# Filter products in high and low halves, vector work moved from GpSimd to VectorE, in a two-layer hybrid backbone

## The chip, the cores and the metric

One core of a Trainium2 chip runs the kernel. The metric is device time in microseconds (us) for one execution, the median of several. The core has TensorE (PE, matmuls; PEld its weight loads), VectorE (DVE), ScalarE (ACT), GpSimd (POOL), and SyncE (SP), which here only issues transfers (DMA). Every engine works off its own instructions in their order and waits for the others on semaphores.

## What is computed

Two layers act on 512 latent and 256 context tokens of 1024 channels. Each layer modulates a norm with vectors computed from a conditioning vector, projects, runs three mixers side by side (a long convolution called Hyena, neighbourhood attention, latent attention "MLA"), projects back, and runs an MLP with squared ReLU. The parts that the change touches:

```python
def _modulation(cond, w_mod, b_mod):
    m = jax.nn.silu(cond) @ w_mod + b_mod
    return jnp.split(m[:, None, :], 6, axis=-1)

def _adaln(h, g, shift, scale):
    return _rms(h, g) * (1.0 + scale) + shift

def _hyena_filters(L, w1, b1, w2, b2, w3, b3, freq):
    ...
    hdn = jnp.sin(freq[0] * (z @ w1.astype(F32) + b1.astype(F32)))
    hdn = jnp.sin(freq[1] * (hdn @ w2.astype(F32) + b2.astype(F32)))
    h = (hdn @ w3.astype(F32) + b3.astype(F32)).reshape(L, HY_ORDER, 2, HY_DIM)
    ...
    h = h * decay[:, None, None, :]
    return h / (jnp.sum(jnp.abs(h), axis=(0, 2), keepdims=True) + EPS)
...
        mx = _modulation(c, w_mod[i], b_mod[i])
        mc = _modulation(c_ctx[None], w_mod[i], b_mod[i])
        px = _adaln(x, g_norm1[i], mx[0], mx[1]) @ w_in[i]
        pc = _adaln(cx, g_norm1[i], mc[0], mc[1]) @ w_in[i]
```

## The kernel before

**Layout and precision.** Activations lie with channels on partitions: `xT` is 8 tiles of 128 channels by 768 tokens (512 latent, then 256 context). Large products are made from high and low halves: `split` (L135) copies a tile to fp32r on ScalarE (L136) and subtracts that from the source on VectorE (L137); `gemm` (L295) and `mm3` (L131 to L133) then run three matmuls, high-high, high-low and low-high. Matmuls on plain f32 tiles run as two recorded passes.

**Order.** A planner orders each engine's instructions by their place in the program and by when it expects them to be ready; generators woven together (`weave`, `fill`) set that place. Pools reserve memory; a tile with `bufs=n` turns over n buffers.

**Start** (from L1164). `filter_hidden` loads its small tables and computes two sine layers for both layers' filters at once, each as one piece of 768 columns (`sin_layer`): ScalarE scales, five VectorE operations reduce the argument, ScalarE takes the sine. SP then issues x (8 transfers), the last filter weight `w3`, the decay and Fourier tables, and 16 blocks of 512 KB of modulation weights (13 buffers). The squares of x are summed between the two sine layers (`sumsq`). Then three things are woven: the rstd and the multiplication of x by it (`norm_x`), `modulation(0, 1)` and `(0, 0)` (scale and shift of the first norm, matmuls L150), and `spectra`, the filters' generator: per 128 tokens a product with `w3` (L372, plain f32, 65 rows), the decay and norm sums on VectorE, ScalarE and GpSimd (L375 to L385), and per filter a Fourier product (L409). After that `norm_h` makes `hh` (ScalarE, L252) and `hl` (VectorE L253, then GpSimd subtracts, L254). The first large product (`mla_in`, L295) and the value projection (`na_v`, L131 to L133) take the rest of `spectra` as filling.

**Attention and the rest of the modulation.** `mla_attend` of layer 0 is woven with `modulation(0, 2)` and `(0, 4)`. The other modulation vectors come from `modulation_rows` (L174): per block of 128x1024 weights, two streams (latent, context). GpSimd multiplies the block by the context row (L189); one step later VectorE multiplies the block by the latent row and sums (L193) and ScalarE sums GpSimd's product (L194). (0,3), the shift of the second norm, (0,5) and all six vectors of layer 1 run in this way, 64 blocks, one per step of the fill: one per output tile m in the output projection (L1355 on), then `MD + 2` = 3 more (L1379), because L1382 needs (0,3) for the first MLP product, and the others inside `mlp`, `FR` of them per ff1 tile of the first chunks and one per pair of ff2 tiles. In the output projection VectorE also adds the gated tile to x (`add_gated`, L1059), which frees TensorE's tile, makes the low half (L1376) and sums squares (L217).

**Layer 1's norm** (`norm_stream`, L257): per tile of one stream VectorE multiplies (L263), ScalarE makes the high half (L264), VectorE the full value (L265), GpSimd the low half (L266). `na_v` of layer 1 waits for it.

## Time and profile before

| | us |
|---|---|
| median of 3 runs | 1859.73 |
| lowest, highest | 1854.02, 1862.49 |
| the profiled execution, whole time | 1861.99 |
| its span in the profile | 1860.1 |
| TensorE busy (share of the span) | 1770.8 (95%) |
| VectorE busy | 1227.3 (66%) |
| ScalarE busy | 807.1 (43%) |
| GpSimd busy | 339.4 (18%) |

The profile is of one execution. Its views used here: busy time by stretch, the instructions of an engine in order of time (equal ones merged), groups of instructions by line, and the list of waits. `out<-in` are the program's names, `xN` a count, and a bracket gives the idle time of the engine before an instruction and what ended it. A busy TensorE is not TensorE at its peak.

### The profile page before, as it was taken

The page shows a single profiled execution, that of the slowest core. Times are in us where ns is not written, and L with a number is a line of the kernel's source. Part 1 is how long each engine was busy: PE and PEld are TensorE (multiplying, and loading weights), DVE is VectorE, ACT ScalarE, POOL GpSimd, SP SyncE. Part 2 cuts the span into 40 slices and gives each one's busy share as a digit, 9 for nine tenths or more (in the row PEclk, how much of TensorE's full clock was granted, in tenths as well). Part 3 has the DMA queues.
Part 4 walks back from the last instruction along what each step waited for, and adds up shares of the span by engine and source line. Part 5 has one row for each costly group of instructions (what it writes and reads, how often), then busy time and mean ns, then how long its engine had stood idle before and what let it go on. Part 6 is the DMA issues. An engine that isn't in the chain of part 4 may idle for free. (4 is left out here: it accounts for less than half of the span.)

```text
span 1860.1 us, 27267 instructions
## 1 busy us (share of the span) xinstructions
PE 1770.8 (95%) x10794; PEld 1504.4 (81%) x10794; DVE 1227.3 (66%) x2111; ACT 807.1 (43%) x1355; POOL 339.4 (18%) x265
## 2 busy tenths in 40 slices
PE   6899988899998999999999999899899999999999
PEld 2688877666686878888888888789677799999997
DVE  5866876766668876665666447887876665555554
ACT  3433425566644643334333224554566652333231
POOL 1523321200043433233322000530300000000000
PEclk9999998999998999999999999899999999999999
DMA  9123423151243333333332222363040023223332
GB/s 339 60 85 134 161 95 101 42 207 56 100 160 126 114 136 130 120 114 136 113 136 102 69 68 88 96 202 132 24 177 24 24 93 100 91 91 95 98 91 79
DMA packets 73246, 205.07 MB, mean 110 GB/s; under 512 B 12540, under 2 KB 24589, under 8 KB 71840
## 3 DMA queue, kind: packets, MB, share of 16 engines
q1 hardware_dynamic: 71520, 198.10, 31.0%
q0 software_dynamic: 1600, 5.24, 0.8%
q8 instruction: 85, 1.39, 0.3%
q14 instruction: 41, 0.34, 0.1%
HBM read 181.30 MB, written 21.23 MB: 109 GB/s over the span
## 5 line engine op out<-in xcount | busy, mean ns | idle before, releaser
L295 PE MATMUL mm<-t,wh 128*128 128x512 f32 (+1 forms) x2496 | 495.2, 319 | 1.9 <-DVE t L1059 1.3
L295 PEld LDWEIGHTS mm<-t,wh 128*128 128x128 f32 x2496 | 373.2, 190 | 38.0 <-issue 2.4
L136 ACT ACTIVATE wh<-wr 128x1024 fp32r<-128x1024 f32 (+2 forms) x176 | 184.6, 1050 | 415.8 <-PE mm L295 394.4
L295 PE MATMUL mm<-t,wl 128*128 128x512 f32 (+1 forms) x1248 | 298.1, 317 | 0.0
L189 POOL TENSOR_TENSOR wmp<-wm,t 128x1024 f32<-128x1024 f32 x64 | 169.5, 2655 | 485.8 <-DMA wm<-in_w_modr_dram 308.8
L137 DVE TENSOR_TENSOR wl<-wr,wh 128x1024 fp32r<-128x1024 f32 (+2 forms) x176 | 228.0, 1296 | 37.3 <-ACT wh L136 33.8
L295 PE MATMUL mm<-ah,wh 128*128 128x512 f32 (+1 forms) x768 | 231.4, 355 | 4.1 <-DVE t L1059 3.5
L295 PE MATMUL mm<-al,wh 128*128 128x512 f32 (+1 forms) x768 | 233.5, 359 | 0.0
L295 PE MATMUL mm<-ah,wl 128*128 128x512 f32 (+1 forms) x768 | 232.0, 356 | 0.0
L1059 DVE SCALAR_TENSOR_TENSOR t<-mm,mods,t 128x512 f32<-128x512 f32 x216 | 135.9, 657 | 134.3 <-PE mm L295 127.5
L295 PEld LDWEIGHTS mm<-t,wl 128*128 128x128 f32 x1248 | 194.7, 189 | 16.5
L193 DVE SCALAR_TENSOR_TENSOR wm<-wm,t 128x1024 f32<-128x1024 f32 x64 | 91.0, 1426 | 102.7 <-POOL wmp L189 102.7
L295 PEld LDWEIGHTS mm<-ah,wh 128*128 128x128 f32 x768 | 126.7, 188 | 28.5 <-DVE t L1059 3.4
L295 PEld LDWEIGHTS mm<-ah,wl 128*128 128x128 f32 x768 | 127.6, 188 | 22.4
L295 PEld LDWEIGHTS mm<-al,wh 128*128 128x128 f32 x768 | 126.4, 188 | 20.2
L194 ACT ACTIVATE wmp<-wmp 128x1024 f32<-128x1024 f32 x64 | 67.9, 1060 | 149.8 <-POOL wmp L189 149.8
L137 DVE TENSOR_TENSOR al<-relu,ah 128x768 fp32r<-128x768 f32 (+1 forms) x64 | 68.2, 1066 | 37.1 <-ACT ah L136 37.1
L447 DVE TENSOR_REDUCE mmx<-mm 128x1 f32<-128x768 f32 (+1 forms) x80 | 67.7, 847 | 32.1 <-PE mm L133 31.5
L452 ACT ACTIVATE msb<-mm,mmx,qrs 128x768 f32<-128x768 f32 (+1 forms) x80 | 72.2, 903 | 25.3 <-DVE mmx L449 21.3
L1370 PE MATMUL mm<-t,wh 128*128 128x512 f32 x320 | 78.1, 358 | 1.6 <-DVE t L1059 1.6
L1023 ACT ACTIVATE mpt<-mm 128x768 f32<-128x768 f32 (+1 forms) x80 | 57.5, 725 | 49.7 <-PE mm L1022 49.6
L136 ACT ACTIVATE ah<-relu 128x768 fp32r<-128x768 f32 (+1 forms) x64 | 47.3, 739 | 63.4 <-DVE relu L1122 63.3
(311 smaller groups left out, 2990.1 us busy)
## 6 DMA issues: line engine op xcount, KB each, us to landing
wr<-in_w_ff_dram SPq DMA_DIRECT2D x128, 512.0 KB, 3.5
wm<-in_w_modr_dram SPq DMA_DIRECT2D x64, 512.0 KB, 4.4
wm<-in_w_mod_dram SPq DMA_DIRECT2D x32, 512.0 KB, 8.0
wr<-in_w_in_t_dram SPq DMA_DIRECT2D x18, 512.0 KB, 3.8
qk<-qk_spill SPq DMA_DIRECT2D x9, 576.0 KB, 6.2
qk_spill<-upk SPq DMA_DIRECT2D x12, 384.0 KB, 3.0
kx<-kk POOLq DMA_DIRECT2D x16, 256.0 KB, 2.5
wr<-in_w_in_qk_dram SPq DMA_DIRECT2D x8, 512.0 KB, 4.0
```

The costliest lines, as they stand in the source:

```text
L136: act.activation(hi, src, AF.Copy)
L137: dve.tensor_sub(lo, src, r32(hi))
L189: pool.tensor_tensor(P[i - MD], W[i - MD], cr[:, 1], ALU.mult)
L193: dve.scalar_tensor_tensor(w, w, 1.0, cr[:, 0], ALU.mult, ALU.mult, accum_out=mods[:, l, v, k, 0:1])
L194: act.activation(pr, pr, AF.Copy, accum_out=mods[:, l, v, k, 1:2])
L295: pe.matmul(out_[:, po:po + b - a], wk[wx], mk[mx][:, a:b], start=(k == 0 and i == 0), stop=(k == nk - 1 and i == 2))
L447: dve.tensor_reduce(mx, src, AX.X, ALU.max, negate=True)
L452: act.activation(sb[:, h, :n], src[:, h, :n], AF.Exp, bias=mx[:, h:h + 1], scale=1.0 if scale is None else scale[:, h:h + 1], accum_out=sm ...
L1023: act.activation(pt[:, 0:nkt, qt * 128:(qt + 1) * 128], tt[:, :nkt * 128].rearrange("p (c q) -> p c q", q=128), AF.Copy)
L1059: dve.scalar_tensor_tensor(xT[:, m, a:b], t[:, a:b], mods[:, l, v, m, s:s + 1], xT[:, m, a:b], ALU.mult, ALU.add)
L1370: pe.matmul(t[:, a:b], ws[wx], half[mx][:, k % 4, a:b], start=(k == ks[0] and i == 0), stop=(k == 7 and i == 2))
```

## The change

- `modulation_rows`: VectorE makes both streams' sums, in two passes over a block; GpSimd and ScalarE have no part. Weights are loaded two blocks ahead (`MD = 2`).
- The shift (0,3) is made during layer 0's `mla_attend`, with a `cond_rows` of its own; the forced steps at L1379 go. `FR` becomes one step per ff1 tile from the second chunk on. The `qk` tile of `mla_attend` has one buffer instead of two.
- Norms: `norm_x` and `norm_h` go; `norm_stream` serves both layers. VectorE multiplies, ScalarE scales in place, and `split` makes both halves.
- Filters: the sine layers run in three pieces of 256 columns. The hidden values of a layer fill one half of 128 rows with their high part and the other with their low part, and `w3` is stacked to match, so a filter product is two fp32r matmuls of 128 rows.
- Start: `w3`, decay and the first Fourier table are loaded ahead of x; the modulation's blocks have 10 buffers; the squares come after the sine layers, woven with `spectra` at 0.5, and the modulation after the rstd, woven at 1.0.

```diff
@@ modulation_rows
-            if item(i - MD):
-                ...
-                pool.tensor_tensor(P[i - MD], W[i - MD], cr[:, 1], ALU.mult)
-            if item(i - MD - 1):
-                ...
-                dve.scalar_tensor_tensor(w, w, 1.0, cr[:, 0], ALU.mult, ALU.mult, accum_out=mods[:, l, v, k, 0:1])
-                act.activation(pr, pr, AF.Copy, accum_out=mods[:, l, v, k, 1:2])
+        for i in range(MD):
+            weights(i)
+        for i, (l, v, k) in enumerate(items):
+            weights(i + MD)
+            w, junk = W.pop(i), p([128, 1024], tag="wmp")
+            for s in range(2):
+                dve.scalar_tensor_tensor(w if s else junk, w, 1.0, cr[:, s], ALU.mult, ALU.mult,
+                                         accum_out=mods[:, l, v, k, s:s + 1])
@@ norm_stream
         for k in range(KD):
-            t = p([128, NT], tag="sq", bufs=2)[:, a:b]
-            g, m = gains[:, l, 0, k, s:s + 1], mods[:, l, 0, k, s:s + 1]
-            dve.tensor_mul(xT[:, k, a:b], xT[:, k, a:b], rb[:, a:b])
-            act.activation(hh[:, k, a:b], xT[:, k, a:b], AF.Identity, bias=m, scale=g)
-            dve.tensor_scalar(t, xT[:, k, a:b], g, m, ALU.mult, ALU.add)
-            pool.tensor_sub(hl[:, k, a:b], t, r32(hh[:, k, a:b]))
+            t, g, m = xT[:, k, a:b], gains[:, l, 0, k, s:s + 1], mods[:, l, 0, k, s:s + 1]
+            dve.tensor_mul(t, t, rb[:, a:b])
+            act.activation(t, t, AF.Identity, bias=m, scale=g)
+            split(hh[:, k, a:b], hl[:, k, a:b], t)
+            yield
-    MD = 1
+    MD = 2
-    FR = (0, 2)
+    FR = 1
@@ filter_hidden
+        n = 256
+        s1 = {}
+        for c in range(4):
+            if c < 3:
+                t = b_tile()[:, 0:n]
+                pe.matmul(t, w1, z[:, c * n:(c + 1) * n], start=True, stop=True)
+                s1[c] = sin_layer(p, t, fb[:, 0:1], hyc, 0, n)
+            if c:
+                cs = slice((c - 1) * n, c * n)
+                t = b_tile()[:, 0:n]
+                pe.matmul(t, w2, s1.pop(c - 1), start=True, stop=True)
+                s2 = sin_layer(p, t, fb[:, 1:2], hyc, 1, n)
+                for l, (a, b) in enumerate(h2):
+                    mine, other, _ = filter_halves(l)
+                    act.activation(a[mine, cs], s2[mine], AF.Copy)
+                    dve.tensor_sub(a[other, cs], s2[mine], r32(a[mine, cs]))
+                    act.activation(b[mine, cs], s2[mine], AF.Copy)
             yield
+    def filter_weights(l, p):
+        ...
+        for x in (mine, other):
+            act.activation(hi[x], raw[mine], AF.Copy)
+        dve.tensor_sub(lo[mine], raw[mine], r32(hi[mine]))
+        act.activation(lo[r:r + 1], raw[r:r + 1], AF.Copy)
+        dve.tensor_sub(lo[r + 32:r + 33], raw[r:r + 1], r32(lo[r:r + 1]))
+        return hi, lo
@@ filter_unit
-                pe.matmul(ph, h2[:, (t0 + tt) * 128:(t0 + tt + 1) * 128], w3[:, o * 512:(o + 1) * 512],
-                          start=True, stop=True)
+                for i in range(2):
+                    pe.matmul(ph, h2[i][:, (t0 + tt) * 128:(t0 + tt + 1) * 128], w3[i][:, o * 512:(o + 1) * 512],
+                              start=(i == 0), stop=(i == 1))
@@ mla_attend
-                QK[hp] = p([128, 2, 6, 192], tag="qk", bufs=2)
+                QK[hp] = p([128, 2, 6, 192], tag="qk")
@@ mlp, ff1
-                for _ in range(FR[c] if c < 2 else 1):
+                for _ in range(FR if c else 0):
@@ start
-    weave((x_in(), 1.0), (chain(modulation(0, 1, wmp, ws=wm1), modulation(0, 0, wmp, ws=wm0)), 1.0), fill=(fill, 1.4))
+    weave((squares_in(), 1.0), fill=(fill, 0.5))
+    next(rstd)
+    weave((chain(modulation(0, 1, wmp, ws=wm1), modulation(0, 0, wmp, ws=wm0)), 1.0), fill=(fill, 1.0))
+    rb = next(rstd)
     wmp.close()
     ...
+    for _ in zip(norm_stream(0, 0, rb, xT, hh, hl, xp), norm_stream(0, 1, rb, xT, hh, hl, xp)):
+        pass
@@ layer 0, attention and output projection
-                  (chain(*[modulation(0, v, wmp) for v in (2, 4)]), 0.2))
+                  (chain(*[modulation(0, v, wmp) for v in (2, 4)]), 0.2),
+                  (modulation_rows([(0, 3)], cond_rows(wmp), wmp), 0.2))
...
-            fill = modulation_rows([(0, 3), (0, 5)] + [(1, v) for v in range(6)], cond_rows(wmp), wmp)
+            fill = modulation_rows([(0, 5)] + [(1, v) for v in range(6)], cond_rows(wmp), wmp)
...
-        if not last:
-            for _ in range(MD + 2):
-                next(fill)
```

## Rows read from the trace of the kernel before

**Rows 1.** Busy time by stretch: us; PE, PEld, DVE, ACT, POOL; PEclk, DMA share, GB/s.
```profile
50.00:55.00 5.00, 5.00 (x34) 2.35 (x33) 3.40 (x11) 1.01 (x2) 2.44 (x2) 1.00 0.00 0
...
75.00:80.00 5.00, 4.67 (x24) 3.75 (x23) 5.00 (x6) 5.00 (x10) 4.41 (x3) 1.00 0.00 0
...
490.00:500.00 10.00, 10.00 (x69) 7.58 (x68) 7.75 (x19) 7.70 (x13) 0.00 (x0) 1.00 0.00 2
...
700.00:750.00 50.00, 50.00 (x286) 43.70 (x285) 32.28 (x45) 21.00 (x32) 16.12 (x6) 1.00 0.35 127
```

**Rows 2.** TensorE in order of time, the start: start us, us, instruction, count.
```profile
34.60 2.08 PE L372 MATMUL b<-w,t 65*128 65x512 f32 x2
...
48.18 1.08 PE L150 MATMUL b<-wm,cst 128*32 128x256 f32 x8
...
58.19 1.07 PE L150 MATMUL b<-wm,cst 128*32 128x256 f32 x16
...
75.51 1.05 PE L295 MATMUL mm<-t,wh 128*128 128x512 f32 x4
...
139.74 1.02 PE L372 MATMUL b<-w,t 65*128 65x512 f32 x2
...
162.91 0.98 PE L295 MATMUL mm<-t,wh 128*128 128x512 f32 x4 [0.54 <-ACT t L489]
```

**Rows 3.** Groups by shape, 0 to 130 us: busy us, mean ns, idle before.
```profile
L254 POOL TENSOR_TENSOR t<-sq,t 128x768 fp32r<-128x768 f32 x8 | 16.3, 2032 | 3.3 <-DVE sq L253 1.8 <-PE b L409 1.6
...
L375 DVE TENSOR_TENSOR h<-b,t 128x512 f32<-128x512 f32 x18 | 12.3, 686 | 7.5 <-PE b L372 5.9 <-POOL sd L385 1.6
L253 DVE TENSOR_SCALAR sq<-t,gains,mods 128x256 f32<-128x256 f32 x8 | 12.0, 1501 | 0.0
...
L339 DVE SCALAR_TENSOR_TENSOR arg<-argk,arg 128x768 f32<-128x768 f32 x4 | 3.8, 954 | 0.1
```

**Rows 4.** TensorE in order of time, end of the output projection.
```profile
573.20 0.93 PE L1370 MATMUL mm<-t,wh 128*128 128x512 f32 x4 [1.62 <-DVE t L1059]
576.07 1.01 PE L1370 MATMUL mm<-t,wl 128*128 128x512 f32 x2 [1.95 <-DVE wl L137]
...
601.50 2.72 PE L224 MATMUL b<-ones,t 128*128 128x1 f32 x12 [5.22 <-DVE t L217]
604.08 1.63 PE L295 MATMUL mm<-t,wh 128*128 128x512 f32 x4
```

**Rows 5.** VectorE, GpSimd and SP in order of time, same stretch.
```profile
558.32 3.42 DVE L193 SCALAR_TENSOR_TENSOR wm<-wm,t 128x1024 f32<-128x1024 f32 x1
...
570.77 1.22 DVE L193 SCALAR_TENSOR_TENSOR wm<-wm,t 128x1024 f32<-128x1024 f32 x1
...
592.77 3.41 DVE L193 SCALAR_TENSOR_TENSOR wm<-wm,t 128x1024 f32<-128x1024 f32 x1 [5.45 <-POOL wmp L189]
...
590.34 4.75 POOL L189 TENSOR_TENSOR wmp<-wm,t 128x1024 f32<-128x1024 f32 x2 [15.41 <-DMA wm<-in_w_modr_dram]
...
576.04 9.70 SPq L280 DMA_DIRECT2D wr<-in_w_ff_dram  x3
```

**Rows 6.** Waits, 540 to 700 us: us in total, times, longest us.
```profile
PE mm L295 <- DVE t L1059: 3.5, 2, 3.1
```

**Rows 7.** Layer 1's norm: TensorE and ScalarE in order of time; L266's durations.
```profile
1168.57 0.29 PE L131 MATMUL mm<-wh,t 128*128 128x288 f32 x1
...
1198.84 3.18 PE L673 MATMUL b<-ones,csq 128*128 128x1 f32 x28
...
1165.88 2.92 ACT L264 ACTIVATE t<-t,mods,gains 128x512 fp32r<-128x512 f32 x4
...
L266 POOL TENSOR_TENSOR t<-sq,t x16: 762/1261/2641, 1166.8 to 1191.1; 128x512 fp32r<-128x512 f32 x8, 128x256 fp32r<-128x256 f32 x8
```

**Rows 8.** The costliest groups (part 5 of the page): one row of VectorE.
```profile
L193 DVE SCALAR_TENSOR_TENSOR wm<-wm,t 128x1024 f32<-128x1024 f32 x64 | 91.0, 1426 | 102.7 <-POOL wmp L189 102.7
```

**Rows 9.** Groups of ScalarE over the span: one row, a table load.
```profile
L171 ACT ACT_TABLE_LOAD x1 | 1.3, 1283 | 0.0
```

More of the change, by code (lines that the diff above doesn't have):

```diff
@@ L176, in modulation_rows, with weights @@
         items = [(l, v, k) for l, v in lv for k in range(KD)]
-        W, P = {}, {}
-        def item(i):
-            return items[i] if 0 <= i < len(items) else None
-        for i in range(len(items) + MD + 2):
-            if item(i):
+        W = {}
+        def weights(i):
+            if i < len(items):
                 l, v, k = items[i]
@@ L350, in filter_hidden @@
[L350 to L360 removed]
+        hyc, fb = load(p, "hy_c", [128, 4]), p([128, 2])
@@ L1165 @@
     fp = Pool("filters", "right")
-    h2 = [fp([65, NT]) for _ in range(DEPTH)]
+    h2 = [(fp([128, NT], F32R), fp([128, NT], F32R)) for _ in range(DEPTH)]
     wmp = Pool("wm_start")
@@ L1239 @@
             sc = Pool(f"mlain{l}", "right")
-            late = norm_rstd(acc, NT, sc), lambda s, rb: norm_stream(l, s, rb, xT, hh, hl, xp)
+            late = norm_rstd(acc, NT, sc), lambda s, rb: list(norm_stream(l, s, rb, xT, hh, hl, xp))
         if l:
```

90 lines of the change are left out of this document (33 added, 57 removed).

## The prediction

> **What bounds the kernel now.** I read the table of busy time by stretch first. TensorE is full almost everywhere: from 700 to 750 us it is busy 50.00 of 50 while VectorE has 32 and GpSimd 16 [rows 1]. Work moved between the vector engines is worth nothing there, so only stretches where TensorE stands still or runs at its low pace count. The list of TensorE's instructions in order of time then gives three such places that the diff touches.
>
> The start: the first large product (L295) begins at 75.51 and the product after the value projection at 162.91 [rows 2]. Before that, TensorE works through the filters' products and the modulation in the order of the program, at low pace: the same L150 matmuls run 8 in 1.08 us at 48 and 16 in 1.07 us at 58 [rows 2]. The column of the granted clock reads 1.00 on both sides [rows 1], so I go by the pace (that of 1.2 and then of 2.4 GHz). Transfers are over by 50 us (none from 50 to 55) [rows 1], so the weights are in long before 75. From 75 to 80 VectorE is busy 5.00 of 5 [rows 1], and its small tensor_scalar (L253, 128x256) takes 1501 ns on average beside GpSimd's subtraction of 2032 [rows 3], longer than a 128x512 operation with two inputs elsewhere (686) [rows 3].
>
> The end of the output projection and the beginning of the first MLP: TensorE waits 1.62 and 1.95 us and then runs two matmuls in 1.01 us, and waits again 5.22 us before the norm's sums, after which four matmuls take 1.63 us instead of 1.05 [rows 4, 2]. In VectorE's list one L193 takes 3.42 us beside GpSimd and 1.22 alone, and at 592.77 it sat 5.45 us at the head of the queue for GpSimd's product, which itself began after 15.41 us of waiting for its block of weights; that transfer stood on SP behind one that held SP from 576.04 for 9.70 us [rows 5]. The gated additions that free TensorE's tiles are queued behind that L193. Later in the same stretch TensorE waits up to 3.1 us more for such an addition (L1059) [rows 6].
>
> Layer 1's norm: between 1168.57 and the short products at 1198.84 stand 30.3 us [rows 7] for 48 x 3 matmuls of 288 columns that follow each other at about 0.13 us, 18.9 us of work. The rest, 11.4 us, is waiting for GpSimd's subtraction, which takes up to 2641 ns [rows 7].
>
> **The change part by part.** *Modulation rows on VectorE.* Removed: 64 GpSimd products and 64 ScalarE sums. Added: a second VectorE pass of 1.22 us per block. The mean pass today is 1426 ns and VectorE idled 102.7 us in front of them for GpSimd [rows 8]. In the output projection and early MLP, 24 blocks lose about 11 us in L193 itself (24 x (1.66 - 1.22), the first and last of them in [rows 5]) and about as much again in the other operations that meet GpSimd there, so 24 x 1.22 = 29 us of new passes cost VectorE 5 to 10 us net, and no wait for GpSimd is left. One block per output tile is 2 x 1.22 + about 4.4 of the other vector work = 6.9 us, below the tile's 8.5 us of matmuls (eight steps of six, about 1.06 us each). What goes: 1.62 + 1.95 + some 3 us of low pace; 5.22 + 1.3 (the sums at low pace) + 2.5 (six-matmul steps at low pace); and 3 to 4 us of the later wait. Together 20 us. What can stay: a pass that waits for its weights directly, since the distance from load to use (two blocks) is unchanged and SP can still be held by a raw-weight load. I take 17 of 20, with bounds 10 and 20.
>
> That first block row (0,3) moves into layer 0's latent attention, so the forced three-block drain ahead of the MLP disappears too. Its price: 8 blocks x 2.5 us = 20 us of VectorE in a stretch where it is busy 7.75 of 10 and TensorE 10.00 of 10 [rows 1], one block in five steps of some 2.4 us. Behind each pair of passes the row maxima are queued, and ScalarE's exponentials, and so TensorE's tiles, wait for those. Also one more 1 MB load and Silu in the middle of the exponentials: two table loads of 1283 ns [rows 9]. The two generators share three weight buffers on one SP queue, and the q/k tile goes from two buffers to one; its refill may start when the last pair's transposes end, some 8 steps ahead of use, so I put that at nothing. Between 0 (all in slack) and -10 (half of the passes on the path) I take -4, nearer to nothing, because VectorE still ends at about 95% of the stretch. In the MLP the remaining 48 blocks add some 7 us of VectorE per 50, covered by TensorE's full 50 [rows 1]; the cost if that cover fails is a rival below.
>
> *Norm without GpSimd.* Per 128x512 piece: VectorE multiply 0.68 (as L375 [rows 3]), ScalarE 0.73 (four L264 in 2.92 [rows 7]) twice, VectorE subtraction 0.68. In layer 1 ScalarE sets the pace, about 1.5 us a tile against 2.1 to 2.6 now, so the latent stream is ready some 5 us earlier and the context stream too. Of the 11.4 us I take 7. The bounds are 11 (all of it) and 3 (the weight blocks behind it come no earlier).
>
> *The start.* Removed on TensorE: a filter product in plain f32 (2.08 us early, 1.02 in the warm stretch [rows 2]) becomes two stacked matmuls of 512 columns: at low pace about 0.9 (from four in 1.63 [rows 4]: each block of 768 columns 0.7), warm 0.46. That is 1.1 us for each of six early products and 0.4 for the rest, some 10 us of TensorE, of which the ten products after 75 us (4 us) are on the path directly. The sine layers in thirds: 30 VectorE operations of 256 columns instead of 10 of 768 (954 for L339 [rows 3], so 0.4 each), 12 us in all against 7.6, plus six copies and subtractions, but three pieces overlap, the squares no longer stand between them, and the filters' tables are first in the queue. The first product can then start at about 17 to 18 us instead of 26, while x lands some 5 us later, which nothing waits for until the rstd. From there VectorE sets the pace: sines 14, splitting the last weight 2.4, squares 7, rsqrt 2, ten products x 2 = 20, one unit's spectrum 4, about 50 us after 8.7, so the shift vector is there near 58 and L295 begins near 60: 15 us earlier. After that the norm's multiply, done beforehand today, lies between: 17 us for the norm (as much as the contended L253 cost), 13 for eight filter steps, 3.6 for weight splits, 34 us on VectorE against 30 on TensorE, so some 5 us come back; one more spectrum group (3.4) lies behind that point, and 4 us of cheaper products are saved. Net 15 - 5 - 3.4 + 4 = 11; with some of the early waits on TensorE gone too I take 14, bounds 4 (L295 starts at 68) and 24 (at 54, nothing given back).
>
> On the port itself the rows say that a VectorE operation with two SBUF inputs stretches to GpSimd's end (3.42 against 1.22 [rows 5]). The Trainium skill, SBUF — State Buffer, "Summary: rules for kernel authors", says the same of two such operations: the second to issue blocks fully until the first ends. By that rule no stretched L193 or L137 is left once GpSimd is idle, which would put the second term at its upper bound, 20.
>
> **Sum.** 14 + 17 + 7 - 4 = 34 us. The profiled execution took 1861.99 us (span 1860.1), so 1828; it lies 2.3 us above the median of the three runs, which puts the median after at 1826. With all bounds at their worst (4 + 10 + 3 - 10 = 7) it is 1853, at their best (24 + 20 + 11 = 55) 1805.
>
> **Rivals.** *The start gives nothing.* VectorE or the modulation's blocks hold L295 near 75 whatever TensorE saves. For it: VectorE is full there already. Against: transfers end by 50 and TensorE's half of the queue shrinks. Sum 20, so 1840.
>
> *TensorE stays at its low pace longer.* Its early work gets thinner, and the pace rose between 48 and 58 us [rows 2], in a stretch in which TensorE was busy 5.00 of 5 [rows 1]. If the rise comes with the large product instead, some 12 us of matmuls run twice as long: 1838. This is also what the Trainium skill makes likely, TensorE: Matmul & The Clock Gate, "Part 1: The HAM clock gate": the throttled state is the default and activity releases it; the rows agree on the rise.
>
> *The waits are not GpSimd's doing.* Then VectorE's passes stay long and double: the second and third terms fall to about 5 together, minus 4, plus 14: 1845.
>
> *Slower: VectorE's queue in the MLP blocks on weights.* A pass at the head of the in-order queue waits for its block and the gated addition behind it is late. GpSimd stood in for that wait so far. There are 48 such blocks; if each stops TensorE by more than 34/48 = 0.7 us, the gain is gone, and at 1.3 us it is 1826 + 62 = 1888. Against it: VectorE waited 102.7 us for GpSimd's products [rows 8] with TensorE at 50.00 of 50 [rows 1], and the direct wait is shorter by the product's 2.4 us.
>
> **How the numbers follow.** The forecast has 0.70, the first rival 0.12, the low pace 0.08, the third 0.05, the slower one 0.05. Two kernels nearer than 0.5% (9 us) can't be told apart in this measurement, so faster means under 1850. The first three cases are nearly all on that side, the third mostly: faster 0.88, same 0.07, slower 0.05. The range takes the bounds of the terms without their joint extremes and the rivals at 1838 to 1845: 1806 to 1850.
>
> **What would show it.** Right: L295 starts near 60 us; no TensorE wait of over 2 us between 560 and 690 (old time) and no L193-like pass over 1.3 us; layer 1's value product done in about 23 us; GpSimd's busy time down by some 200 us; VectorE's up by some 70. Wrong: L295 after 68; waits for L1059 or the row maxima in attention adding to over 10 us; a VectorE pass with long waits for the weights and TensorE idle behind it in the MLP.

## The result and the profile after

The changed kernel takes 1844.55 us (median; 1843.03 to 1847.51), the kernel before 1860.03 beside it on the same chip. The ratio is 0.9919, 95% interval 0.9903 to 0.9936: some 15 us less, where I had forecast 34. The profiled execution has a span of 1841.2 us against 1860.1.

The page's busy times and its two rows for the passes over the modulation weights (columns: busy us, mean ns, idle before; line numbers of the changed kernel, where L193 is L191, L295 is L273, L1059 is L1067, L452 is L460 and L1022 is L1030):

```profile
PE 1753.6 (95%) x10798; PEld 1505.4 (82%) x10798; DVE 1244.3 (68%) x2276; ACT 765.5 (42%) x1285; POOL 142.1 (8%) x183
...
L191 DVE SCALAR_TENSOR_TENSOR wmp<-wm,t 128x1024 f32<-128x1024 f32 x64 | 78.3, 1224 | 65.8 <-DMA wm<-in_w_modr_dram 65.7
...
L191 DVE SCALAR_TENSOR_TENSOR wm<-wm,t 128x1024 f32<-128x1024 f32 x64 | 78.1, 1220 | 0.2
```

GpSimd lost 197 us. VectorE gained only 17: 64 more passes are 78 us, but a pass takes 1.22 us now instead of 1.43 [rows 8], and other operations that met GpSimd shrank too (L137 on 128x1024 tiles, from 1305 to 1223 ns on average).

To see where the time went I cut both executions at the same instructions of TensorE's list. The last column is after minus before; its sum is the difference of the spans but for 0.3 us at the end.

| stretch, us | before | after | difference |
|---|---|---|---|
| start to the first score product of layer 0 (kh,qh) | 378.6 | 375.8 | -2.8 |
| from there to the first output-projection matmul | 132.2 | 142.0 | +9.8 |
| from there to the first ff2 product | 154.7 | 137.6 | -17.1 |
| from there to layer 1's value product | 503.1 | 498.1 | -5.0 |
| layer 1's value product to its last eviction | 33.8 | 30.9 | -2.9 |
| from there to the last ff2 product | 653.5 | 652.3 | -1.2 |

**The start.** TensorE in order of time, as [rows 2]:

```profile
38.93 2.72 PE L221 MATMUL b<-ones,t 128*128 128x1 f32 x12 [12.43 <-DVE t L214]
41.58 1.93 PE L150 MATMUL b<-wm,cst 128*32 128x256 f32 x16
...
65.86 1.08 PE L150 MATMUL b<-wm,cst 128*32 128x256 f32 x8
...
74.15 0.82 PE L232 MATMUL b<-ident,rs 128*128 128x128 f32 x6
```

The norm's sums (L221) stand ahead of all modulation matmuls (L150) in TensorE's queue and wait 12.43 us for VectorE's last square. The spreading of the rstd (L232) comes at 74, behind the modulation and three spectrum groups (L417, 16 matmuls each). The first large product starts at 78.4, later than the 75.51 of [rows 2].

Busy time by stretch, before and then after (columns as in [rows 1]):

```profile
0.00:40.00 40.00, 23.47 (x78) 9.33 (x82) 23.11 (x43) 15.77 (x22) 5.15 (x11) 1.00 0.94 350
40.00:80.00 40.00, 36.09 (x192) 21.91 (x184) 31.98 (x57) 17.64 (x31) 15.36 (x14) 0.96 0.26 93
80.00:120.00 40.00, 37.19 (x203) 30.53 (x204) 29.38 (x48) 11.03 (x19) 19.44 (x19) 1.00 0.28 90
```

```profile
0.00:40.00 40.00, 10.83 (x25) 6.25 (x26) 28.20 (x60) 22.92 (x41) 12.09 (x17) 0.85 0.72 276
40.00:80.00 40.00, 36.91 (x247) 24.92 (x247) 25.61 (x63) 13.35 (x25) 9.26 (x12) 0.85 0.55 187
80.00:120.00 40.00, 39.55 (x223) 34.11 (x222) 34.42 (x68) 27.46 (x49) 11.19 (x13) 0.96 0.21 71
```

In a stretch of fixed length idle time grows by what busy time loses, so I count up to the value product, which starts at 122.0 us before and at 118.9 after: TensorE is busy 86.1 us instead of 98.8, and idle 32.7 instead of 23.3. Of 12.7 us of work saved, 9.4 came back as waiting. VectorE's work in the first 120 us did not shrink: 84.5 before, 88.2 after.

**The attention.** TensorE's waits over 1.5 us in it, and ScalarE just ahead of the first of them:

```profile
384.49 1.51 PE L1030 MATMUL mm<-ident,msb 128*128 128x128 f32 x6 [3.93 <-ACT msb L460]
...
395.69 0.84 PE L1030 MATMUL mm<-ident,msb 128*128 128x128 f32 x6 [2.13 <-DVE msb L468]
...
448.15 0.87 PE L1030 MATMUL mm<-ident,msb 128*128 128x128 f32 x6 [1.85 <-DVE ql L994]
```

```profile
376.95 1.28 ACT L171 ACT_TABLE_LOAD   x1
378.24 1.91 ACT L171 ACTIVATE t<-t 128x2048 f32<-128x2048 f32 x1
380.06 1.04 ACT L136 ACTIVATE wh<-wr 128x1024 fp32r<-128x1024 f32 x1
381.12 1.28 ACT L460 ACT_TABLE_LOAD   x1
382.41 0.99 ACT L460 ACTIVATE msb<-mm,mmx,qrs 128x768 f32<-128x768 f32 x1
```

The Silu of the new conditioning rows and two table loads, 4.5 us, lie directly ahead of the first exponential.

**Output projection and MLP.** The whole list of TensorE's waits from 555 to 1153 us is one line:

```profile
PE mm L273 <- DVE t L1067: 1.3, 1, 1.3
```

Before, [rows 4] and [rows 6] alone held 12.3 us of such waits.

**Layer 1's norm.** TensorE, then busy time of two stretches:

```profile
1164.09 0.40 PE L131 MATMUL mm<-wh,t 128*128 128x288 f32 x1 [2.94 <-ACT t L136]
1164.91 5.97 PE L681 MATMUL b<-ones,csq 128*128 128x1 f32 x28
```

```profile
1150.00:1160.00 10.00, 10.00 (x72) 9.58 (x71) 9.96 (x21) 10.00 (x17) 0.00 (x0) 1.00 0.01 1
1160.00:1170.00 10.00, 7.06 (x38) 6.83 (x36) 4.08 (x10) 10.00 (x23) 1.42 (x2) 0.72 0.07 20
```

No wait for GpSimd is left, but ScalarE is now busy 10.00 of 10 through both stretches. The one wait, 2.94 us for ScalarE's high half, stands ahead of the short products: they take 5.97 us where [rows 7] shows 3.18, with a granted clock of 0.72.

### The profile page after: what moved, and what is told of

It is laid out like the page before. It is cut to its first block, busy times and chain, and to the rows that moved or that the text cites. A ratio compares the mean times of both kernels' runs of the same rounds, so it can differ in the third digit from the quotient of the medians.

```text
span 1841.2 us, 27122 instructions
## 1 busy us (share of the span) xinstructions
PE 1753.6 (95%) x10798; PEld 1505.4 (82%) x10798; DVE 1244.3 (68%) x2276; ACT 765.5 (42%) x1285; POOL 142.1 (8%) x183
## 5 line engine op out<-in xcount | busy, mean ns | idle before, releaser
L273 PE MATMUL mm<-t,wh 128*128 128x512 f32 (+1 forms) x2496 | 490.6, 317 | 2.2 <-DVE t L1067 1.3
L273 PEld LDWEIGHTS mm<-t,wh 128*128 128x128 f32 x2496 | 371.5, 189 | 37.0 <-ACT wh L136 1.6
L273 PE MATMUL mm<-t,wl 128*128 128x512 f32 (+1 forms) x1248 | 298.1, 317 | 0.0
L137 DVE TENSOR_TENSOR wl<-wr,wh 128x1024 fp32r<-128x1024 f32 (+2 forms) x176 | 213.6, 1214 | 35.6 <-ACT wh L136 30.4
L273 PE MATMUL mm<-al,wh 128*128 128x512 f32 (+1 forms) x768 | 233.5, 359 | 0.0
L273 PE MATMUL mm<-ah,wl 128*128 128x512 f32 (+1 forms) x768 | 232.1, 356 | 0.0
L1067 DVE SCALAR_TENSOR_TENSOR t<-mm,mods,t 128x512 f32<-128x512 f32 x216 | 136.3, 659 | 140.6 <-PE mm L273 133.4
L273 PE MATMUL mm<-ah,wh 128*128 128x512 f32 (+1 forms) x768 | 230.9, 354 | 0.0
L273 PEld LDWEIGHTS mm<-t,wl 128*128 128x128 f32 x1248 | 194.1, 189 | 16.1
L273 PEld LDWEIGHTS mm<-ah,wl 128*128 128x128 f32 x768 | 127.6, 188 | 22.5
L273 PEld LDWEIGHTS mm<-ah,wh 128*128 128x128 f32 x768 | 126.8, 188 | 23.5
L273 PEld LDWEIGHTS mm<-al,wh 128*128 128x128 f32 x768 | 126.2, 188 | 20.1
L191 DVE SCALAR_TENSOR_TENSOR wmp<-wm,t 128x1024 f32<-128x1024 f32 x64 | 78.3, 1224 | 65.8 <-DMA wm<-in_w_modr_dram 65.7
L460 ACT ACTIVATE msb<-mm,mmx,qrs 128x768 f32<-128x768 f32 (+1 forms) x80 | 72.2, 903 | 24.6 <-DVE mmx L457 18.3
L1120 DVE TENSOR_SCALAR bb<-mm,cols 128x2 f32<-128x2 f32 x64 | 14.1, 220 | 98.2 <-PE mm L273 97.5
L191 DVE SCALAR_TENSOR_TENSOR wm<-wm,t 128x1024 f32<-128x1024 f32 x64 | 78.1, 1220 | 0.2
L137 DVE TENSOR_TENSOR al<-relu,ah 128x768 fp32r<-128x768 f32 (+1 forms) x64 | 52.6, 823 | 36.2 <-ACT ah L136 36.1
L1379 PE MATMUL mm<-t,wh 128*128 128x512 f32 x320 | 75.1, 348 | 0.0
```

The source lines that it names most:

```text
L137: dve.tensor_sub(lo, src, r32(hi))
L191: dve.scalar_tensor_tensor(w if s else junk, w, 1.0, cr[:, s], ALU.mult, ALU.mult, accum_out=mods[:, l, v, k, s:s + 1])
L273: pe.matmul(out_[:, po:po + b - a], wk[wx], mk[mx][:, a:b], start=(k == 0 and i == 0), stop=(k == nk - 1 and i == 2))
L460: act.activation(sb[:, h, :n], src[:, h, :n], AF.Exp, bias=mx[:, h:h + 1], scale=1.0 if scale is None else scale[:, h:h + 1], accum_out=sm ...
L1067: dve.scalar_tensor_tensor(xT[:, m, a:b], t[:, a:b], mods[:, l, v, m, s:s + 1], xT[:, m, a:b], ALU.mult, ALU.add)
L1379: pe.matmul(t[:, a:b], ws[wx], half[mx][:, k % 4, a:b], start=(k == ks[0] and i == 0), stop=(k == 7 and i == 2))
```

## The experiments

All ratios are to the kernel before, timed beside each; it took 1861.4 to 1866.5 us there, and 1860.0 beside the change, so the whole times of different runs are compared by the ratios. The attention's length is always that from the first score product to the first output-projection matmul. My theory was: the rows without GpSimd bring what was forecast; the start's gain is eaten by the order of TensorE's queue; the attention costs more than forecast because of the Silu or of the passes. Rivals: the start is bound elsewhere, and the waits are not GpSimd's doing.

### The parts one by one on the kernel before

The rows alone (`modulation_rows` as in the diff of the change, in the kernel before):

```diff
-    MD = 1
+    MD = 2
@@ behind the output projection
-        if not last:
-            for _ in range(MD + 2):
-                next(fill)
```

> The kernel before with one part of the change: modulation rows as two VectorE passes per block, weights two blocks ahead, no forced steps ahead of the MLP; the shift (0,3) stays in the output projection, start, norms and attention are those of before. Theory (GpSimd's part was the cause of the waits): from the first output-projection matmul to the first ff2 product 138 us instead of 154.7, from there to layer 1's value product 498 instead of 503, time 1838 to 1842. Rival (the waits are not GpSimd's doing): 1850 to 1860.

Measured: 1841.29 us, ratio 0.9872 (0.9848 to 0.9895). Projection to first ff2 product 138.9 us, from there to layer 1's value product 498.1, layer 1's value product 34.0. Theory right: these rows, with GpSimd out of them, are worth 154.7 + 503.1 - 138.9 - 498.1 = 20.8 us. The ratio's 24 us hold a little more than the profile shows. No pass is stretched any more (1228 ns at most, 3426 before). The run takes out GpSimd's product, ScalarE's sum and the three forced steps together, so what each of the three is worth is not shown. VectorE's passes in the same stretch (520 to 700 us):

```profile
L191 DVE SCALAR_TENSOR_TENSOR wmp<-wm,t 128x1024 f32<-128x1024 f32 x28 | 34.2, 1220 | 12.2 <-DMA wm<-in_w_modr_dram 12.2
```

They do wait for their weights, 12.2 us, and TensorE doesn't stand behind them.

The rows and layer 1's norm:

```diff
-            act.activation(hh[:, k, a:b], xT[:, k, a:b], AF.Identity, bias=m, scale=g)
-            dve.tensor_scalar(t, xT[:, k, a:b], g, m, ALU.mult, ALU.add)
-            pool.tensor_sub(hl[:, k, a:b], t, r32(hh[:, k, a:b]))
+            act.activation(t, t, AF.Identity, bias=m, scale=g)
+            split(hh[:, k, a:b], hl[:, k, a:b], t)
```

> As the run with the rows alone, and layer 1's norm without GpSimd as in the change. It differs from the changed kernel with the shift in the projection (1830.6) in the start alone. Theory (the start is worth some 3 us, the norm 4): 2 to 5 us below the rows alone and 2 to 4 us above that kernel, 1833 to 1837. Rival (the start is worth nothing): 1829 to 1832.

Measured: 1836.94 us, 0.9849 (0.982 to 0.9878). The value product of layer 1 takes 30.9 us instead of 34.0, so the norm is worth 3 us. The rest differs by what kernels of one start differ by (below).

The same with one buffer for the q/k tile:

```diff
-                QK[hp] = p([128, 2, 6, 192], tag="qk", bufs=2)
+                QK[hp] = p([128, 2, 6, 192], tag="qk")
```

> The kernel before with rows, norm and a single buffer for the q/k tile of the attention; it differs from the changed kernel with the shift in the projection in the start alone. Theory (the second q/k buffer costs 4 us: from the first score product kh,qh to the first output-projection matmul the kernels with one buffer took 128.4 us and those with two 132.3): 128 to 129 us there, and the whole time within 2 us of 1830, so that the new start is worth nothing. Rival (the 4 us belong to the new start, whose first products or clock carry into the attention): 132 to 133 us there, the time 1833 to 1837.

Measured: 1836.64 us, 0.9848 (0.9828 to 0.9869), attention 131.2 us. Both readings missed. It is 1.0 us less than with two buffers, and some 0.6 of that is no gain: ten of the 128 modulation matmuls L150 of this stretch run ahead of the first score product here (an estimate, from 16 in 1.07 us [rows 2]). So the buffer is worth next to nothing. The start has no part in it either: 131.3 appears with the new start too, and what the 128.4 of the other kernel is shows in TensorE's pace, below.

### The attention

The shift back in the projection:

```diff
-                  (chain(*[modulation(0, v, wmp) for v in (2, 4)]), 0.2),
-                  (modulation_rows([(0, 3)], cond_rows(wmp), wmp), 0.2))
+                  (chain(*[modulation(0, v, wmp) for v in (2, 4)]), 0.2))
...
-            fill = modulation_rows([(0, 5)] + [(1, v) for v in range(6)], cond_rows(wmp), wmp)
+            fill = modulation_rows([(0, 3), (0, 5)] + [(1, v) for v in range(6)], cond_rows(wmp), wmp)
...
-    FR = 1
+    FR = (0, 2)
...
-                for _ in range(FR if c else 0):
+                for _ in range(FR[c] if c < 2 else 1):
```

> The changed kernel with the shift (0,3) taken out of layer 0's attention and put back as the first 8 blocks of the fill of the output projection, one block per tile; (0,5) then takes two blocks per ff1 tile of the second chunk, as before. Still two VectorE passes per block and no GpSimd. Theory (the passes, the Silu and the load in attention cost 9.7 us there, and GpSimd was the cause of the waits behind): first output-projection matmul near 508 instead of 517.7, no wait over 2 us ahead of the MLP's first products, time 1835 to 1838. Rival (the shift's last passes and its high and low halves then hold up the first MLP): 2 to 6 us of it come back there, 1839 to 1843.

Measured: 1830.62 us, 0.9837 (0.9815 to 0.9859). The attention takes 128.4 us instead of 142.0, and the projection to the first ff2 product 138.9 instead of 137.6. So moving the shift into the attention costs 13.6 us, and this kernel beats the changed one and the one before. The 1.3 us are no saving of the move: 137.6 and 138.9 both occur with the shift in either place, and TensorE waits in none of them. Of the 13.6 us, 7.3 are more idle time of TensorE in the attention (10.7 instead of 3.3) and 6.3 more busy time for the same matmuls but the ten named above, at a granted clock of 0.96 instead of 1.00. From the projection to layer 1 TensorE has one wait, of 1.3 us; no forced step is needed, since the eight blocks end with the eight tiles.

Only the load and the Silu in the attention (the rest as in the last run):

```diff
-                  (modulation_rows([(0, 3)], cond_rows(wmp), wmp), 0.2))
+                  (iter([cond_rows(wmp)]), 0.2))
```

> As the run with (0,3) back in the projection, but the load of the conditioning rows and their Silu stay at the beginning of the attention (no use is made of them there; the projection makes its own). Theory (the Silu between two table loads, 4.5 us of ScalarE right ahead of the first exponential, with the fall of TensorE's pace behind it): at least half of the 9.7 us stays, first output-projection matmul at 513 to 516. Rival (the 16 passes ahead of row maxima and reciprocals): it starts within 2 us of the run without the Silu, near 508 to 510.

Measured: 1837.68 us, 0.9868 (0.9841 to 0.9895), attention 133.8. ScalarE and TensorE there:

```profile
379.89 1.28 ACT L171 ACT_TABLE_LOAD   x1
381.19 1.91 ACT L171 ACTIVATE t<-t 128x2048 f32<-128x2048 f32 x1
...
384.06 1.28 ACT L460 ACT_TABLE_LOAD   x1
```

```profile
387.44 1.51 PE L1030 MATMUL mm<-ident,msb 128*128 128x128 f32 x6 [3.92 <-ACT msb L460]
```

The first wait of the changed kernel (3.93 us for the first exponential) is there with the Silu alone. It is worth 5.4 us of the 13.6 (2.6 against the kernels in which TensorE's pace falls there anyway, see below), the passes the other 8.2. The passes' weights are not the reason: in the changed kernel's attention VectorE waits 0.9 us for them in all.

The Silu ahead of the neighbourhood attention, the passes in place:

```diff
+        if not last:
+            rp = Pool("rows0")
+            cr0 = cond_rows(rp)
         mp = Pool(f"mixa{l}")
...
-                  (modulation_rows([(0, 3)], cond_rows(wmp), wmp), 0.2))
+                  (modulation_rows([(0, 3)], cr0, wmp), 0.2))
...
+        if not last:
+            rp.close()
```

> The changed kernel with the conditioning rows of the attention's shift loaded and put through their Silu before the neighbourhood attention, instead of at the beginning of the latent attention; the 16 passes stay there. Theory (the Silu's place costs 5.4 us, the passes 8.2): from the first score product to the first output-projection matmul 136 to 138 us instead of 142.0, time 1838 to 1841. Rival (both only keep VectorE and ScalarE late together, and the passes alone cost all of it): 140 to 142 us, 1843 to 1846.

Measured: 1843.31 us, 0.9881 (0.9857 to 0.9905), attention 138.1: 3.9 us less than the changed kernel, at the edge of the theory's range; the whole time is 7 us less by the ratios. Whether part of the Silu has only moved is not shown: the first score product comes at 381.4 us, against 375.8 to 378.7 without it there, which is within the variation of one start (below).

The passes spread out, with the Silu ahead (the shift's passes pinned to their place in the program):

```diff
-                dve.scalar_tensor_tensor(w if s else junk, w, 1.0, cr[:, s], ALU.mult, ALU.mult,
-                                         accum_out=mods[:, l, v, k, s:s + 1])
+                pass_ = dve.scalar_tensor_tensor(w if s else junk, w, 1.0, cr[:, s], ALU.mult, ALU.mult,
+                                                 accum_out=mods[:, l, v, k, s:s + 1])
+                if (l, v) == (0, 3):
+                    pin(pass_)
```

> As the run with the Silu ahead (attention 138.1 us from the first score product to the first output-projection matmul), and the 16 passes of the shift keep their place in the program, two in about 24 VectorE instructions, instead of being drawn forward. Theory (the cost is the crowding: row maxima and reciprocals stand behind several passes): 130 to 133 us there, time 4 to 8 us below that run's. Rival (each pass on VectorE delays the block behind it, 8 blocks of about 1 us each, wherever they stand): 136 to 139 us, same time.

Measured: 1849.06 us, 0.9914 (0.9896 to 0.9932), attention 142.3. The passes' rows (duration min/median/max, first and last start), for the Silu ahead and for this one:

```profile
L191 DVE SCALAR_TENSOR_TENSOR wmp<-wm,t x8: 1205/1218/1226, 389.5 to 440.6; 128x1024 f32<-128x1024 f32 x8
```

```profile
L191 DVE SCALAR_TENSOR_TENSOR wmp<-wm,t x8: 1208/1216/1219, 397.4 to 497.3; 128x1024 f32<-128x1024 f32 x8
```

They run from 397 to 497 us now instead of 389 to 441, and it costs 4 us more, not less. My theory (crowding) falls. Against 131.2 us without them, 8 blocks cost 11.1 us, 1.4 each, a little more than one pass, though VectorE is idle a fourth of the time. TensorE's idle time in the attention is 12.3 us instead of 3.4, nearly all of it for VectorE's and ScalarE's results. The reading that fits is that each pair delays the block of softmax rows queued behind it, wherever it stands; no run isolates it.

TensorE's pace there, for the shift in the projection and then for the run with the multiplications beside the modulation (next section), whose attention has the same code:

```profile
380.00:390.00 10.00, 7.47 (x60) 5.54 (x60) 8.63 (x18) 5.70 (x10) 0.00 (x0) 1.00 0.90 321
```

```profile
380.00:390.00 10.00, 7.47 (x44) 5.89 (x38) 7.23 (x16) 4.25 (x8) 0.00 (x0) 0.72 0.84 294
```

TensorE is busy 7.47 of 10 in both, with two gaps (1.42 and 1.10 us; 1.18 and 1.35). In the first the granted clock stays at 1.00, in the second it falls to 0.72, and the attention is 128.4 against 131.3 us. So 2.9 us of the 13.6 are the luck of that profile: 131.3 is as much the time of this code as 128.4. In the changed kernel the 3.93 us gap brings 0.66 in the same stretch.

### The start

First the variation: up to the attention the changed kernel, the one with the shift in the projection and the one with the Silu alone have the same code, and the first score product starts at 375.8, 378.4 and 378.7. The kernels with the start of before have it at 378.6, 380.7, 374.9 and 376.3, so one profile can differ by 6 us from another of the same start. Both means are 377.6. The value product varies too (117.8 to 122.0 with the start of before, 118.9 to 121.3 with the new one). The new start is worth nothing that shows. The whole times agree: rows, norm and buffer with the start of before have 0.9848, the kernel with the shift in the projection, which differs in the start and its norm alone, 0.9837, and the intervals overlap.

| run | first large product | value product | first score product |
|---|---|---|---|
| before | 75.5 | 122.0 | 378.6 |
| after | 78.4 | 118.9 | 375.8 |
| shift in the projection | 80.0 | 120.4 | 378.4 |
| (0,1) first | 70.9 | 129.5 | 386.1 |
| (0,1) and rstd first | 69.7 | 118.3 | 378.0 |
| filters behind the norm | 69.4 | 122.4 | 386.6 |
| multiply beside modulation | 72.0 | 120.8 | 377.2 |
| one pass on ScalarE | 72.0 | 127.9 | 383.3 |
| no filter sums | 74.1 | 115.8 | 371.1 |
| no sum of squares | 77.4 | 116.5 | 372.3 |

The scale (0,1) ahead of the rstd sums:

```diff
-    weave((squares_in(), 1.0), fill=(fill, 0.5))
+    weave((squares_in(), 1.0), (modulation(0, 1, wmp, ws=wm1), 0.5), fill=(fill, 0.5))
     next(rstd)
-    weave((chain(modulation(0, 1, wmp, ws=wm1), modulation(0, 0, wmp, ws=wm0)), 1.0), fill=(fill, 1.0))
+    weave((modulation(0, 0, wmp, ws=wm0), 1.0), fill=(fill, 1.0))
     rb = next(rstd)
```

> The changed kernel with one edit: the matmuls of modulation (0,1) are woven with the squares, ahead of the rstd sums in TensorE's order, instead of behind them; the rest as it is. Theory (TensorE's queue ate the start's gain: it stands 12.4 us in front of the rstd sums L221 with the modulation's blocks long landed, and all of the modulation behind it): first L150 near 24 us instead of 41.6, the modulation over by 57 instead of 66.9, the first large product L273 at 64 to 70 instead of 78.4, time 1835 to 1840. Rival (VectorE's work ahead of the norm sets that point, whatever TensorE's order): L273 at 75 to 78, time 1842 to 1846.

Measured: 1854.62 us, 0.9955 (0.9938 to 0.9972). L150 starts at 22.9 and the first large product at 70.9, and yet it is slower than the changed kernel, by 7 us by the ratios. Neither reading has that. TensorE, then two stretches:

```profile
70.92 2.93 PE L273 MATMUL mm<-t,wh 128*128 128x512 f32 x8 [1.07 <-ACT t L136]
81.97 1.01 PE L273 MATMUL mm<-t,wl 128*128 128x512 f32 x2 [8.13 <-DVE wl L137]
```

```profile
70.00:80.00 10.00, 2.93 (x8) 2.25 (x8) 9.97 (x21) 10.00 (x21) 1.46 (x1) 0.50 0.00 0
80.00:90.00 10.00, 8.03 (x35) 6.61 (x36) 9.22 (x17) 6.38 (x13) 1.45 (x1) 0.72 0.31 88
```

The product has started, but the low half of its weight is queued on VectorE behind the norm: VectorE and ScalarE are full, TensorE stands 8.13 us, and the granted clock is at 0.50, the lower level of 1.2 GHz.

With the spreading of the rstd ahead of (0,0) as well:

```diff
+    shift = modulation(0, 0, wmp, ws=wm0)
+    next(shift)
     rb = next(rstd)
+    weave((shift, 1.0), fill=(fill, 1.0))
```

> As the run with (0,1) woven with the squares, and the transposes that spread the rstd (L232) are put ahead of modulation (0,0), so that VectorE can multiply x by it before the shift is there. Theory (the queue's order): the multiplications L241 start by 60 and L273 at 60 to 66, another 2 to 4 us earlier: 1831 to 1838. Rival (VectorE is full anyway, the multiplications only change place with filter work): no more than 1 us from the run without it.

Measured: 1847.52 us, 0.9924 (0.9901 to 0.9947). The first large product comes 8.6 us earlier than in the changed kernel, the value product 0.5 us, and the whole time is that of the changed kernel. Both readings missed: it is better than the run before by 6 us, and not better than the change. The wait ahead of the norm's sums is gone, and another of the same size is there:

```profile
41.91 0.69 PE L158 MATMUL b<-ident,wr 128*128 128x128 f32 x2 [10.90 <-ACT wr L155]
```

The filters behind the norm (on the kernel with the shift in the projection, with the order of the last run):

```diff
-    weave((squares_in(), 1.0), (modulation(0, 1, wmp, ws=wm1), 0.5), fill=(fill, 0.5))
+    weave((squares_in(), 1.0), (modulation(0, 1, wmp, ws=wm1), 0.5), fill=(fill, 0.0))
...
-    weave((shift, 1.0), fill=(fill, 1.0))
+    weave((shift, 1.0), fill=(fill, 0.5))
...
-    MF, VF = 0.5, 0.4
+    MF, VF = 0.8, 0.6
```

> The changed kernel with the shift in the projection (1830.6) and another start: (0,1) woven with the squares without any filter step, the spreading of the rstd ahead of (0,0), the filters at half a step beside (0,0), the rest of them as filling of the first large products at 0.8 and 0.6 instead of 0.5 and 0.4. Theory (VectorE's filter work ahead of the norm holds up the first products): L273 near 60, value product at 108 to 114 instead of 120, time 1820 to 1826. Rival (the filters' VectorE work is only moved behind, and TensorE waits for it there): value product no earlier than 117, time 1829 to 1838.

Measured: 1841.1 us, 0.987 (0.985 to 0.9891). Rival right, and worse: TensorE waits 14.2 us for a weight's high half ahead of its first large product, then never 1 us until 170, and is 8 us late at the first score product. Its work is only put off, and the wait is lost.

The multiplications beside the modulation (on the kernel with the shift in the projection):

```diff
-            dve.tensor_mul(t, t, rb[:, a:b])
+            if l:
+                dve.tensor_mul(t, t, rb[:, a:b])
...
-    weave((chain(modulation(0, 1, wmp, ws=wm1), modulation(0, 0, wmp, ws=wm0)), 1.0), fill=(fill, 1.0))
+    scale = modulation(0, 1, wmp, ws=wm1)
+    next(scale)
     rb = next(rstd)
+    def x_in():
+        for k in range(KD):
+            dve.tensor_mul(xT[:, k], xT[:, k], rb)
+            yield
+    weave((chain(scale, modulation(0, 0, wmp, ws=wm0)), 1.0), (x_in(), 1.0), fill=(fill, 1.0))
```

> The changed kernel with the shift in the projection (1830.6), the spreading of the rstd put ahead of the modulation's second step and the multiplications of x by it woven with the modulation, where VectorE idled 14 of 30 us, instead of at the head of the norm. Theory (after the shift, VectorE's and ScalarE's norm work, 16 and 18 us in one stretch, sets when the products can stream): value product 3 to 6 us earlier, at 114 to 117 instead of 120.4, time 1824 to 1828. Rival (ScalarE's two passes alone set it, 18 us): value product within 2 us of 120, time 1829 to 1832.

Measured: 1833.68 us, 0.9829 (0.9806 to 0.9853): first large product 8 us earlier, value product the same, time the same. The rival's value product holds.

In addition one pass on ScalarE, two on VectorE, in layer 0's norm:

```diff
-            act.activation(t, t, AF.Identity, bias=m, scale=g)
-            split(hh[:, k, a:b], hl[:, k, a:b], t)
+            if l:
+                ...
+            else:
+                u = p([128, NT], tag="sq", bufs=2)[:, a:b]
+                act.activation(hh[:, k, a:b], t, AF.Identity, bias=m, scale=g)
+                dve.tensor_scalar(u, t, g, m, ALU.mult, ALU.add)
+                dve.tensor_sub(hl[:, k, a:b], u, r32(hh[:, k, a:b]))
```

> As the run with the multiplications beside the modulation, and in layer 0's norm ScalarE makes the high half directly (one pass), VectorE the full value and the low half (two passes), as before but without GpSimd. Theory (ScalarE's 18 us set the norm): value product another 2 to 4 us earlier, 1821 to 1826. Rival (VectorE's passes set it, and it gets one more): 1 to 4 us later than without it.

Measured: 1836.39 us, 0.9849 (0.9827 to 0.9872), value product 7 us later (the rival had 1 to 4), with a wait of 4.31 us for a weight's low half (VectorE). So ScalarE's passes alone are not the bound: VectorE's queue in the norm is at least as late.

Two removals from VectorE, each on the changed kernel. The filters' sums of absolute values left out (the filters' norm is then that of the first 128 tokens):

```diff
                     act.activation(ab, h, AF.Abs)
-                    dve.tensor_add(acc, acc, ab)
```

> The changed kernel without the 12 additions of L391 in the filters (0.965 us each, VectorE; the norm of a filter is then that of its first 128 tokens, so the filters are scaled wrongly). Theory (VectorE's work ahead of the norm sets when the input products can stream): value product 6 to 10 us earlier, at 109 to 113 instead of 118.9, time 1835 to 1839. Rival (TensorE's own work at its low pace sets it): value product within 2 us of 118.9, time within 3 us of 1844.6.

Measured: 1840.81 us, 0.9871 (0.9848 to 0.9893). Value product 3.1 us earlier, first score product 4.7 (6.5 against the mean): about half of the 11.6 us that are gone, and between the two readings. By the ratios the whole time is 9 us less than the changed kernel's.

The sums of the squares of x left out at the start (layer 0's norm is then that of the first 128 channels):

```diff
-            dve.tensor_add(acc, acc, sq)
+            if xT is not x_start:
+                dve.tensor_add(acc, acc, sq)
```

> The changed kernel without the seven additions of the squares of x at the start (L214, 0.94 us each; the first norm is then that of the first 128 channels). Theory (VectorE's chain of sines and squares ahead of the rstd sets the start): rstd sums at about 32 instead of 38.9, the value product 5 to 7 us earlier, 112 to 114, first score product at 369 to 371, time 1836 to 1840. Rival (the work behind the rstd sets it, the first modulation matmuls only wait elsewhere): value product within 2 us of 118.9, time within 3 us of the changed kernel.

Measured: 1840.61 us, 0.9877 (0.9855 to 0.9899). The rstd sums move from 38.9 to 27.8, more than the theory had, and the value product by 2.4 us, nearer to the rival:

```profile
27.84 2.55 PE L222 MATMUL b<-ones,t 128*128 128x1 f32 x12
...
63.12 1.84 PE L401 MATMUL b<-ones,facc 128*128 128x1 f32 x8 [3.90 <-DVE facc L392]
...
72.23 0.82 PE L233 MATMUL b<-ident,rs 128*128 128x128 f32 x6
```

Of 11 us won at the sums, 1 is left at the first large product (77.4): the last modulation matmuls stand behind a filter's sum that waits 3.9 us for VectorE, and the rstd is still spread behind them all. The first score product comes 3.5 us earlier, and by the ratios the whole time is 8 us less than the changed kernel's.

## Why the prediction was off

**Modulation rows: 17 forecast (10 to 20), 22 measured, 20.8 with the rows alone.** 17.1 us up to the first ff2 product and 5.0 behind it, where the step had put 20 in all up to 690 us. No pass over 1.3 us is left, no wait over 2 us. The mechanism was right, the size a little above its upper bound. (The pass begun at 592.77 does not stretch to GpSimd's end, as the step has it: it ends at 596.18, 1.1 us behind GpSimd's products, which end at 595.09 [rows 5].) The rule of the Trainium skill, SBUF — State Buffer, "Summary: rules for kernel authors", had put the term at that bound; the trace agrees with it so far that with GpSimd idle no stretched pass is left, and 1.22 us for each is what the row shows. What I had kept back, a pass that waits directly for its weights, came (65.8 us of idle time ahead of the passes), and TensorE has one wait of 1.3 us from the projection to layer 1. With that the slower rival falls, and so does the one by which VectorE's passes stay long.

**Norm: 7 forecast (3 to 11), 3 measured.** The step that failed is the reading of 11.4 us as waiting for GpSimd's subtraction. TensorE before, three of its waits among the 144 matmuls:

```profile
1177.41 0.41 PE L133 MATMUL mm<-wh,t 128*128 128x288 f32 x1 [2.34 <-POOL t L266]
...
1181.77 0.40 PE L131 MATMUL mm<-wh,t 128*128 128x288 f32 x1 [1.26 <-ACT t L264]
...
1183.47 0.61 PE L133 MATMUL mm<-wh,t 128*128 128x288 f32 x1 [1.18 <-POOL t L266]
```

All waits from 1168.57 to 1198.84 are 6.7 us, 4.2 of them for GpSimd; the other 4.7 of the 11.4 are matmuls at a lower pace (granted clock 0.89 there). Of the 6.7, 2.94 are left. ScalarE sets the pace as the step said: the latent tiles' passes (1.51 and 1.14 us for two) share ScalarE with other work (L671, L673, L729), and the context tiles come 2.94 us late. Behind that wait the short products run at a granted clock of 0.72 and give back 2.8 us.

**Attention: +4 forecast (0 to 10), +9.8 measured against before, 13.6 against the same kernel without it.** The mechanism was named and the value was not: I took it near nothing because VectorE would end at some 95% of the stretch. It ended at 75% (106.6 of 142.0 us), and the passes cost 8.2 us all the same. The failed step is to hold a busy share against a queue in which each block waits for the one before: a block costs 1.0 us in the changed kernel and 1.4 with the passes spread. That the queue is the reason is argued, as said above. And the Silu had no term of its own, though its parts were known from [rows 9]; it took 5.4 us, 2.2 of idle time of TensorE and 3.2 of busy time (some 0.6 for the ten matmuls, the rest at the lower pace behind the gap).

**Start: -14 forecast (-4 to -24), 0 measured.** This is most of what is missing: the start 14, the attention 6 and the norm 4 fell short, the rows gave 5 more, 19 in all. (The span fell short of the forecast by 15 only: in this pair of profiles the start is 2.8 earlier, within what one program shows, and the rest of layer 1 is 1.2 shorter.) The step that failed is "the first product begins near 60, 15 earlier" as a measure of the gain. First, the order of TensorE's queue put the modulation behind the rstd sums, which I had not seen, and it began at 78.4. But that is not the cause: four other orders brought it to 69 to 72, and none brought the value product below 118.3. The saving on TensorE was there (12.7 us of busy time up to the value product), and 9.4 us of it came back as idle time; the 3 us that are left are within what one start varies by. My working let VectorE's sum end at 58 with VectorE at work all the time; in the trace VectorE idles 14 us between 40 and 80 and the norm then needs VectorE and ScalarE both, with the weights' low halves in the same queues.

The rival "the start gives nothing" (1840) is the one whose number came true, and with the attention's 6 us beyond the forecast it gives 1846 (the norm's 4 and the rows' 5 nearly cancel). Its mechanism did not quite: the first large product was not held near 75 whatever TensorE did, since its place in the queue alone moved it from 78 to 70, but the value product came no earlier for it. Not settled is which of VectorE's, ScalarE's and the modulation's chains is last in the start: two removals of 6.6 and 11.6 us of VectorE gave 3.5 and 4.7 us up to the first score product and 8 and 9 us of whole time by the ratios, no order gave any, and both removals together were not tried. That TensorE stays at its low pace longer is not so by the pace of equal matmuls: 16 of L150 take 1.07 us from 46.70 on, where before 8 took 1.08 at 48.18 [rows 2].

```profile
46.70 1.07 PE L150 MATMUL b<-wm,cst 128*32 128x256 f32 x16
...
54.87 3.72 PE L417 MATMUL b<-sd,t 128*128 128x256 f32 x16
...
69.21 5.10 PE L417 MATMUL b<-sd,t 128*128 128x256 f32 x16
```

It falls once more at 65.86, behind a wait of 2.22 us, and the spectrum group at 69.21 is 1.4 us longer for it. The column of the granted clock (0.85 from 0 to 80 us, 1.00 and 0.96 before) can't be compared here, since it read 1.00 over the slow matmuls of before too.

## What to carry to other kernels

Measure an earlier start at the point where all the work that was to be done by then is done, not at the first instruction that moves: if TensorE waits for VectorE, cheaper matmuls become idle time. A share of 75% busy is no slack where each piece of a pipeline waits for the last one: eight blocks of extra passes cost 1.0 to 1.4 us each there, while 48 in the MLP left TensorE one wait of 1.3 us. Put a function that needs a table load away from the first use of another, and leave a step in the place that already hides it: the change without its move into the attention is some 15 us faster than the change by the ratios.

## What was unexpected of the hardware

Two gaps of TensorE, 1.42 and 1.10 us, left the granted clock at 1.00 in one execution, and two of 1.18 and 1.35 brought 0.72 in another with the same busy time (7.47 of 10); the six transposes behind the second gap took 0.85 us in the one and 1.51 in the other. The same code stands in five profiles with nearly the same gaps: in three the clock stayed at 1.00 and the attention took 128.4, 128.3 and 128.4 us, in two it fell and the attention took 131.3 and 131.2. The gaps of 3.93, 3.92 and 2.94 us shown above were followed by 0.66, 0.72 and 0.72. The two falls whose price can be read cost 2.9 us (the attention) and 2.8 us (the short products), as much as a gap.
